# Where gate block 6's adding DMA stands in a hybrid encoder block, and the order in which two PSUM pools open

## The chip, the cores and the metric

The kernel runs on one core of one Trainium2 chip. The metric is the device time of one execution in microseconds (us); less is better. The engines are TensorE (PE, with its weight loads shown apart as PEld), VectorE (DVE), ScalarE (ACT), GpSimd (POOL) and SyncE (SP). Each works through its own list of instructions in order, and waits on semaphores where it needs something of another engine or of a DMA. SP, ACT and POOL also issue DMAs; in the trace the issuing of a DMA from SP or ACT has a lane with a q (SPq, ACTq).

## The reference: what is computed

One layer of an encoder block on x of 512 frames by 1024 channels, all in 32-bit floats. An input projection feeds two token mixers and their gates; then come an output projection, a layer norm, a gated feed-forward network with a causal convolution, and a second layer norm. Cut to what matters here:

```python
proj = x @ w_in[layer]
q_a, k_a, v_a, q_i, k_i, w_i, q_s, k_s, v_s, g_a, g_b = jnp.split(proj, IN_OFFSETS, axis=-1)
y_a = ... # sparse attention: an indexer picks 256 keys per query, 8 heads
y_s = ... # stick-breaking attention, 8 heads
gate_a = jax.nn.sigmoid(g_a + b_gates[layer, 0])
gate_b = jax.nn.sigmoid(g_b + b_gates[layer, 1])
merged = gate_a * (y_a @ w_branch_dsa[layer]) + gate_b * (y_s @ w_branch_sb[layer])
x = layer_norm(DEEPNORM_ALPHA * x + merged @ w_out[layer], ln1_g[layer], ln1_b[layer])
u, g = jnp.split(x @ w_ffn_in[layer], 2, axis=-1)
h = jax.nn.gelu(causal_dwconv(u, conv_w[layer], conv_b[layer])) * g
x = layer_norm(DEEPNORM_ALPHA * x + h @ w_ffn_out[layer], ln2_g[layer], ln2_b[layer])
```

## The kernel before

**Precision.** PE multiplies in a rounded format. So every 32-bit operand is split into a high half (rounded) and a low half (the rest), and every product is three matmuls: high by high, low by high, high by low. For a projection block of 128 output channels (`proj_t`, lines 230 to 232) that makes 24 matmuls: eight chunks of the input channels, and for each L230 (x high by weight high), L231 (x low by weight high) and L232 (x high by weight low).

**Splitting the weights.** The class `Stream` runs through one list of weight pieces (`order`), each 128 by 1024 numbers or 512 KB. SP loads a piece into one of three `raw` buffers (L72), ACT copies it rounded into `whi` (L103), and the low half `wlo` comes about in one of three ways. DVE or POOL subtracts (L110); or, for the 14 pieces listed in `DMA_LO`, ACT writes the negated high half into `wlo` (L106, "the negated half") and POOL then issues a DMA that loads the same piece once more from memory and adds it onto that (L107, "the adding DMA"). `whi` and `wlo` have three buffers each. Gate blocks 4, 5, 6 and 7 (gb4 to gb7, pieces 28 to 31) are done in this third way; so `wlo_30` is gate block 6's low half and `wlo_31` is gate block 7's.

**The attention stage** lasts from about 60 to 330 us. The two mixers' heads run one after the other: stick-breaking heads 0 to 7, then sparse heads 0 to 7. A head's own matmuls are few, and its chain on the other engines is long, so PE is filled between them with the projection blocks in the order of `FILL`: ... qa0 ka0 gb4 gb5 gb6 gb7 qa1 ka1 va ... For a stick-breaking head, PE makes `z_ps` (L530), ACT takes two sigmoids, `keep` and `beta` (L534, L535), DVE runs a reversed running product over `keep` (L544, "the sticks"), and POOL multiplies `beta` by it (L547, "the head's product"). From head 4 on the weights are turned round by DMA: ACT and POOL write the two 16-bit halves of `beta` into `keep` (L466, L467), SP issues two transposing DMAs into `pl` (L469), POOL and ACT put the halves together in `back` (L478, L479), ACT and DVE split that into `pth` and `ptl` (L481, L485), and PE multiplies these by the values (`av_ps`, L501). Beside this DVE works through the top-256 selection for the sparse heads (L420, L421, `score`). A sparse head starts with `l_ps` (L570).

**What sets the order.** The instructions are handed to a scheduler that simulates a timeline and fixes the order of each engine's list; `tc.issue_after(x)` ties what is issued inside it to come after instruction x in that order. Four ties stand around the change. POOL's product of a head is tied behind the adding DMA last recorded in `st.added` for head 5 alone (`behind=i == TURN + 1`, TURN being 4). ACT's copies of ka0 (`stack_hl`, L335 and L336) are tied behind `pth` of head 4 (`firsts[0]`). `Stream.behind` makes one coming high half wait for that same `pth`; that is gate block 6's. The sigmoid of gate block 4 (L627) has no tie.

**The last two PSUM pools.** PSUM has eight banks; pool `psB` holds banks 0 to 3 throughout, and `psA` holds 4 to 7 until the first two blocks of the feed-forward stage are done. These are u_ps and g_ps of blocks 0 and 1, made by `ffn_in` and read by `activate` (ACT copies u_ps, L964; DVE multiplies g_ps by the activated c, L977). Then `psA` is closed and its four banks go to two new pools, each tile waiting for what last stood in its own bank: `psC` (u_ps and g_ps of blocks 2 to 21) takes 4 and 5, and `psD` (the sums P0 and P1, L1001 to L1003) takes 6 and 7.

## Time and profile before

| what | value |
|---|---|
| timed runs of the kernel before | 752.59, 752.68, 753.98 us; median 752.68 |
| the profiled execution's own time | 753.88 us |
| its span, first to last instruction | 752.1 us |
| mean granted TensorE clock over the span | 0.994 |
| PE busy | 739.6 us, 98% of the span |
| DVE, ACT, POOL busy | 569.3, 406.4, 149.5 us |
| issue to landing of the 14 adding DMAs, median | 7.1 us |

Times on the profile's page and in the trace count from the start of the span. A row of the timeline reads: start in us, duration in us, engine, line, operation, out<-in, shape, number of instructions merged; in square brackets at its end stands how long the engine sat idle before it and what ended that. The waits view gives the total, the number and the longest of the waits of one kind. The windows view gives, for each stretch, its length and each engine's busy time in it (with the number of instructions), then the granted TensorE clock as a share of full speed, the DMA engines' mean share and GB/s. "DMA to landing" is the time from issue until a DMA's semaphore tells that all has landed, as minimum, median and maximum of those in the window.

### The profile page before, as it was taken

What the parts mean: (1) busy time and instruction counts of PE and PEld (TensorE: products, weight loads), DVE (VectorE), ACT (ScalarE), POOL (GpSimd) and SP (SyncE); (2) the same over time, 40 slices, a digit from 0 to 9 for tenths busy, and PEclk for the clock granted to TensorE, in tenths of its full rate; (3) what the DMA queues carried; (4) which work ended last, traced back from release to release, by engine and by line L of the source; (5) the groups of instructions that cost most, each with busy time, mean ns of one, the idle gap of its engine ahead of it and who ended that gap; (6) DMA issues with size and microseconds to landing.
All of it is one profiled execution on the core that took longest, in us unless ns stands there. A gap on an engine that the chain in (4) does not pass through costs nothing.

```text
span 752.1 us, 9760 instructions
## 1 busy us (share of the span) xinstructions
PE 739.6 (98%) x3485; PEld 619.5 (82%) x3485; DVE 569.3 (76%) x907; ACT 406.4 (54%) x572; POOL 149.5 (20%) x161
## 2 busy tenths in 40 slices
PE   9999999998999999999999999999999999999995
PEld 7877888886888888888889888888888888888885
DVE  5569788998579999658774967676776668668995
ACT  5465767795786588746374534443443344346430
POOL 1001224374742432000011111011101101110011
PEclk9999999999999999999999999999999999999998
DMA  8445887796556455327732444435343444448532
GB/s 268 151 127 183 190 183 170 151 203 162 133 152 161 122 146 118 121 61 231 303 60 75 170 143 158 146 114 167 125 159 136 140 141 143 141 146 290 198 117 84
DMA packets 71008, 116.38 MB, mean 155 GB/s; under 512 B 39913, under 2 KB 40169, under 8 KB 70961
## 3 DMA queue, kind: packets, MB, share of 16 engines
q1 hardware_dynamic: 63680, 93.33, 41.1%
q0 software_dynamic: 5744, 18.38, 9.7%
q10 hardware_dynamic: 1536, 4.06, 2.2%
q8 instruction: 27, 0.44, 0.3%
q14 instruction: 21, 0.16, 0.1%
HBM read 95.93 MB, written 9.98 MB: 141 GB/s over the span
## 4 chain that ended last, share of the span: by engine, by line
PE 92%; DVE 4%; DMA 1%; issue 1%; ACT 1%; POOL 0%; DVEq 0%; POOLq 0%; ACTq 0%
PE u_ps L922 5%; PE u_ps L921 5%; PE g_ps L922 5%; PE u_ps L923 5%; PE g_ps L921 5%; PE g_ps L923 5%; PE m L1002 2%; PE m L1001 2%; PE m L1003 2%; PE av_ps L501 2%; PE ga_ps L232 2%; PE ga_ps L231 2%; PE ga_ps L230 2%; PE o_ps L852 2%; PE o_ps L851 2%; PE o_ps L850 2%
## 5 line engine op out<-in xcount | busy, mean ns | idle before, releaser
L103 ACT ACTIVATE whi<-raw 128x1024 fp32r<-128x1024 f32 (+1 forms) x124 | 124.0, 1002 | 158.7 <-PE g_ps L922 45.9
L110 DVE TENSOR_TENSOR wlo<-raw,whi 128x1024 fp32r<-128x1024 f32 (+1 forms) x105 | 124.3, 1185 | 40.4 <-ACT whi L103 39.5
L923 PE MATMUL u_ps<-x1h,wlo 128*128 128x512 f32 (+1 forms) x192 | 71.4, 372 | 0.0
L921 PE MATMUL u_ps<-x1h,whi 128*128 128x512 f32 (+1 forms) x192 | 71.3, 372 | 0.0
L922 PE MATMUL u_ps<-x1l,whi 128*128 128x512 f32 (+1 forms) x192 | 71.3, 371 | 0.0
L921 PE MATMUL g_ps<-x1h,whi 128*128 128x512 f32 (+1 forms) x184 | 69.9, 380 | 0.0
L922 PE MATMUL g_ps<-x1l,whi 128*128 128x512 f32 (+1 forms) x184 | 69.9, 380 | 0.0
L923 PE MATMUL g_ps<-x1h,wlo 128*128 128x512 f32 (+1 forms) x184 | 69.9, 380 | 0.0
L921 PEld LDWEIGHTS u_ps<-x1h,whi 128*128 128x128 f32 x192 | 36.2, 188 | 6.3
L922 PEld LDWEIGHTS u_ps<-x1l,whi 128*128 128x128 f32 x192 | 36.2, 188 | 6.2
L923 PEld LDWEIGHTS u_ps<-x1h,wlo 128*128 128x128 f32 x192 | 36.2, 188 | 6.2
L921 PEld LDWEIGHTS g_ps<-x1h,whi 128*128 128x128 f32 x184 | 34.6, 188 | 6.6
L923 PEld LDWEIGHTS g_ps<-x1h,wlo 128*128 128x128 f32 x184 | 34.6, 188 | 6.5
L922 PEld LDWEIGHTS g_ps<-x1l,whi 128*128 128x128 f32 x184 | 34.6, 188 | 6.5
L944 DVE TENSOR_TENSOR t<-raw 128x512 f32<-128x512 f32 x11 | 7.6, 692 | 40.0 <-DMA raw<-in_w_fo_dram 39.6
L559 POOL TENSOR_TENSOR bm<-win,score 128x256 f32<-128x256 f32 (+2 forms) x24 | 26.0, 1112 | 32.2 <-DMA pl<-bm 16.1
L963 POOL MEMSET u<- 128x2 f32 x22 | 2.1, 98 | 145.0 <-ACT whi L103 101.2
L977 DVE TENSOR_TENSOR hF<-g_ps,c 128x512 f32<-128x512 f32 x22 | 15.1, 686 | 20.8 <-PE g_ps L923 20.8
L969 ACT ACTIVATE c<-c,cwt 128x512 f32<-128x512 f32 x22 | 15.9, 725 | 25.2 <-DVE c L968 25.0
L819 POOL TENSOR_TENSOR rstd<-rstd,mhalf 128x1 f32<-128x1 f32 x8 | 7.7, 958 | 104.4 <-DVE rstd L818 104.4
L232 PE MATMUL gb_ps<-xh,wlo 128*128 128x512 f32 x64 | 25.7, 404 | 2.6 <-DMA wlo<-in_w_t_dram 2.6
L420 DVE MAX8 m<-score 128x8 f32<-128x256 f32 (+2 forms) x48 | 26.5, 554 | 1.7 <-DMA pl<-keep 0.8
(578 smaller groups left out, 2085.2 us busy)
## 6 DMA issues: line engine op xcount, KB each, us to landing
raw<-in_w_fi_dram SPq DMA_DIRECT2D x44, 512.0 KB, 3.3
raw<-in_w_t_dram SPq DMA_DIRECT2D x32, 512.0 KB, 3.5
raw<-in_w_fo_dram SPq DMA_DIRECT2D x26, 512.0 KB, 4.1
wlo<-in_w_t_dram POOLq DMA_DIRECT2D x14, 512.0 KB, 7.1
raw<-in_w_br_dram SPq DMA_DIRECT2D x8, 512.0 KB, 4.0
raw<-in_w_o_dram SPq DMA_DIRECT2D x8, 512.0 KB, 4.4
raw<-in_w_v_dram SPq DMA_DIRECT2D x7, 512.0 KB, 3.8
raw_b<-in_w_fo_dram SPq DMA_DIRECT2D x6, 512.0 KB, 5.3
```

Of the source, the lines that this page charges most:

```text
L103: self.high = nc.scalar.activation(hi[:, :w], t[:, :w], AF.Copy).ins
L110: self.done[key] = eng.tensor_sub(lo[:, :w], t[:, :w], r32(hi[:, :w])).ins
L230: nc.tensor.matmul(ps[:M], wh[:, c], xh[k], start=(k == 0), stop=False)
L231: nc.tensor.matmul(ps[:M], wh[:, c], xl[k], start=False, stop=False)
L232: nc.tensor.matmul(ps[:M], wl[:, c], xh[k], start=False, stop=(k == KC - 1))
L420: nc.vector.max(m8, sc)
L559: nc.gpsimd.tensor_add(bm[:, OFF[j]:OFF[j] + N], win[:, 512 - N:512], score[j])
L921: nc.tensor.matmul(ps[:, c], wh[:, kc], x1h[:, k, c], start=(k == 0), stop=False)
L922: nc.tensor.matmul(ps[:, c], wh[:, kc], x1l[:, k, c], start=False, stop=False)
L923: nc.tensor.matmul(ps[:, c], wl[:, kc], x1h[:, k, c], start=False, stop=(k == KC - 1))
L969: nc.scalar.activation(c, c, AF.Gelu_apprx_tanh, bias=cwt[:, f, 3:4])
L977: nc.vector.tensor_mul(F[:, o:o + 2].rearrange("p a b -> p (a b)"), gps_, c)
```

## The change

`Stream` now keeps every negated half in `st.highs`, by piece. ACT's copies of ka0 and its sigmoid of gate block 4 are tied behind gate block 6's negated half, instead of ka0's copies behind head 4's `pth`. The high half after gate block 6's (gate block 7's) is tied behind that negated half too. POOL's product of head 5 is tied behind gate block 5's adding DMA, which is the same DMA as before; the product of head 6 is newly tied behind gate block 6's adding DMA. And `psD` is opened ahead of `psC`, and closed after it.

```diff
@@ class Stream
+        self.highs = {}
...
             if key in self.lo_by_dma:
-                self.high = nc.scalar.activation(lo[:, :w], r32(hi[:, :w]), AF.Copy, scale=-1.0).ins
-                self.done[key] = self.added = nc.gpsimd.dma_start(lo[:, :w], self.pieces[self.ns][1], accum_op=ALU.add).ins
+                self.high = self.highs[key] = nc.scalar.activation(lo[:, :w], r32(hi[:, :w]), AF.Copy, scale=-1.0).ins
+                if key == "gb6":
+                    self.behind = self.high
+                self.done[key] = nc.gpsimd.dma_start(lo[:, :w], self.pieces[self.ns][1], accum_op=ALU.add).ins
@@ sb_sticks
-    def sb_sticks(beta, keep, behind=False):
+    def sb_sticks(beta, keep, behind=None):
...
-        with tc.issue_after(st.added) if behind else nullcontext():
+        with tc.issue_after(st.done[behind]) if behind else nullcontext():
             nc.gpsimd.tensor_mul(beta, beta, keep[:, 1:ATT + 1])
@@ filler
             elif kind in ("ks", "ka"):
-                with tc.issue_after(firsts[0]) if t == "ka0" and firsts else nullcontext():
+                with tc.issue_after(st.highs["gb6"]) if t == "ka0" and firsts else nullcontext():
                     qk[t] = stack_hl(ps, "k", 4, t)
             elif kind == "gb":
                 g = xp.tile([128, 512], F32, tag="m", bufs=8, name=t)
-                ups[t] = nc.scalar.activation(g, ps, AF.Sigmoid, bias=bgt[:, 8 + n:9 + n]).ins
+                with tc.issue_after(st.highs["gb6"]) if n == 4 else nullcontext():
+                    ups[t] = nc.scalar.activation(g, ps, AF.Sigmoid, bias=bgt[:, 8 + n:9 + n]).ins
@@ advance
-        last = sb_sticks(*following, behind=i == TURN + 1)
+        last = sb_sticks(*following, behind={TURN + 1: "gb5", TURN + 2: "gb6"}.get(i))
@@ tile_block
     close(ac)
+    psd, psD = open_pool("psD", space=PSUM, reuse_waits="tile")
     psc, psC = open_pool("psC", space=PSUM, reuse_waits="tile")
-    psd, psD = open_pool("psD", space=PSUM, reuse_waits="tile")
...
+    close(psc)
     close(psd)
-    close(psc)
```

The ties move instructions on all five engines between about 160 and 240 us; before and behind that stretch the lists are the same but for a few DVE and ACT rows in the last 50 us. No instruction is added or removed. The line numbers of the changed kernel are up to four higher. The numbers behind the names tell buffers apart: `_30_` is gate block 6's piece and `_31_` gate block 7's, beta_1642 and keep_1643 are stick-breaking head 6's, pl_1574 and back_1718 head 5's planes, pl_1713 head 6's planes, pth_1839 and av_ps_1980 head 6's turned weights and their product.

The first place is ACT's list where gate block 6 is split, before:

```order
L103 ACTIVATE whi_30_1624<-raw_30_1622 128x1024
L335 ACTIVATE ka0a_1676<-ka0_ps_1629 64x512
L336 ACTIVATE ka0b_1677<-ka0_ps_1629 64x512
L103 ACTIVATE whi_31_1684<-raw_31_1682 128x1024
L627 ACTIVATE gb4_1755<-gb4_ps_1689,bgt_105 128x512
L106 ACTIVATE wlo_30_1625<-whi_30_1624 128x1024
L106 ACTIVATE wlo_31_1685<-whi_31_1684 128x1024
```

and in the change:

```order
L104 ACTIVATE whi_30_1624<-raw_30_1622 128x1024
L107 ACTIVATE wlo_30_1625<-whi_30_1624 128x1024
L338 ACTIVATE ka0a_1676<-ka0_ps_1629 64x512
L339 ACTIVATE ka0b_1677<-ka0_ps_1629 64x512
L104 ACTIVATE whi_31_1684<-raw_31_1682 128x1024
L631 ACTIVATE gb4_1755<-gb4_ps_1689,bgt_105 128x512
L107 ACTIVATE wlo_31_1685<-whi_31_1684 128x1024
```

Gate block 6's negated half passes the four instructions that stood between it and its high half; gate block 7's keeps its place behind gate block 4's sigmoid. POOL's list at the same place, before:

```order
L467 COPY keep_1525<-beta_1524 128x1280
L547 TENSOR_TENSOR beta_1642<-beta_1642,keep_1643 128x1280
L107 DMA wlo_30_1625<-in_w_t_dram 128x1024
L107 DMA wlo_31_1685<-in_w_t_dram 128x1024
L467 COPY keep_1643<-beta_1642 128x1280
L479 COPY back_1718<-pl_1574 128x1280
```

and in the change:

```order
L470 COPY keep_1525<-beta_1524 128x1280
L110 DMA wlo_30_1625<-in_w_t_dram 128x1024
L550 TENSOR_TENSOR beta_1642<-beta_1642,keep_1643 128x1280
L110 DMA wlo_31_1685<-in_w_t_dram 128x1024
L482 COPY back_1718<-pl_1574 128x1280
L470 COPY keep_1643<-beta_1642 128x1280
```

Gate block 6's adding DMA passes head 6's product; gate block 7's stays behind it. The second place is SP's list, which issues the loads and the transposing DMAs, before:

```order
L72 DMA raw_33_1857<-in_w_t_dram 128x1024
L72 DMA raw_34_1890<-in_w_v_dram 128x1024
L469 DMA_TRANSPOSE pl_1574<-keep_1525 128x10x128
L554 DMA win_2056<-s_win 128x512
L72 DMA raw_35_1924<-in_w_v_dram 128x1024
L72 DMA raw_36_2006<-in_w_v_dram 128x1024
L469 DMA_TRANSPOSE pl_1713<-keep_1643 128x10x128 x2
```

and in the change:

```order
L73 DMA raw_33_1857<-in_w_t_dram 128x1024
L472 DMA_TRANSPOSE pl_1574<-keep_1525 128x10x128
L73 DMA raw_34_1890<-in_w_v_dram 128x1024
L557 DMA win_2056<-s_win 128x512
L472 DMA_TRANSPOSE pl_1713<-keep_1643 128x10x128
L73 DMA raw_35_1924<-in_w_v_dram 128x1024
L472 DMA_TRANSPOSE pl_1713<-keep_1643 128x10x128
L73 DMA raw_36_2006<-in_w_v_dram 128x1024
```

Head 5's second transpose passes one load, and head 6's two pass two loads and one load. The third place is PE's list in the values of the sparse mixer (va_ps, 128 by 512 each), where head 6's turned weights are used; before, twenty-one matmuls of va stand ahead of the row of av_ps, of which these are the last:

```order
L269 MATMUL va_ps2_2094<-whi_34_1892,xl1_186 128x512
L267 MATMUL va_ps1_2093<-whi_35_1926,xh2_227 128x512
L267 MATMUL va_ps2_2094<-whi_35_1926,xh2_227 128x512
L501 MATMUL av_ps_1980<-pth_1839,vs0_704 128x384
L570 MATMUL l_ps_2067<-ka0b_1677,qa0b_1617 128x512 x2
L501 MATMUL av_ps_1980<-ptl_1840,vs0_704 128x384
```

and in the change seven:

```order
L271 MATMUL va_ps1_2093<-wlo_34_1893,xh0_131 128x512
L272 MATMUL va_ps1_2093<-whi_34_1892,xl0_132 128x512
L270 MATMUL va_ps0_2092<-whi_34_1892,xh1_185 128x512
L504 MATMUL av_ps_1980<-pth_1839,vs0_704 128x384
L573 MATMUL l_ps_2067<-ka0b_1677,qa0b_1617 128x512 x2
```

Head 6's product with the values passes fourteen matmuls of va. In the built programs the banks of the feed-forward stage differ too: before, u_ps and g_ps of block 1 stand in banks 4 and 5, block 2's u_ps in 4, and P0 and P1 in 6 and 7; in the change, u_ps and g_ps of block 1 stand in banks 5 and 4, block 2's u_ps in 6 (which block 0's u_ps had), and P0 and P1 in 4 and 5.

## The prediction

> **What bounds the kernel now.** I read the page's busy shares and its chain of waits first, then PE's waits, then the timeline at the longest of them.

> ```profile
> PE 739.6 (98%) x3485; PEld 619.5 (82%) x3485; DVE 569.3 (76%) x907; ACT 406.4 (54%) x572; POOL 149.5 (20%) x161
> ...
> PE 92%; DVE 4%; DMA 1%; issue 1%; ACT 1%; POOL 0%; DVEq 0%; POOLq 0%; ACTq 0%
> ```

> PE is busy for 98% of the span. So an edit that adds or removes no matmul can only move what is left: the stretches in which PE stands or runs slowly. The view of PE's waits lists all of them:

> ```profile
> PE gb_ps L232 <- DMA wlo<-in_w_t_dram: 2.6, 1, 2.6
> ...
> PE dot_ps L403 <- ACT relu L406: 1.0, 1, 1.0
> ```

> The one wait of 2.6 us is on the low half of gate block 6. PE's timeline there:

> ```profile
> 170.28 0.39 PE L230 MATMUL gb_ps<-xh,whi 128*128 128x512 f32 x1
> 170.50 0.39 PE L231 MATMUL gb_ps<-xl,whi 128*128 128x512 f32 x1
> 173.46 0.80 PE L232 MATMUL gb_ps<-xh,wlo 128*128 128x512 f32 x1 [2.57 <-DMA wlo<-in_w_t_dram]
> ...
> 176.19 0.60 PE L232 MATMUL gb_ps<-xh,wlo 128*128 128x512 f32 x1
> 176.61 0.41 PE L230 MATMUL gb_ps<-xh,whi 128*128 128x512 f32 x1
> ```

> Starts of such matmuls lie 0.22 to 0.23 us apart (170.28 to 170.50). The L232 that starts at 173.46 would have started at 170.73, so 2.73 us are lost. The seven matmuls from 173.46 to 176.61 take 3.15 us instead of 7 x 0.227 = 1.59, another 1.56 us. The windows view says why:

> ```profile
> 52.00:54.00 2.00, 0.98 (x8) 0.79 (x7) 1.90 (x3) 2.00 (x5) 0.00 (x0) 1.00 0.57 154
> ...
> 170.50:173.40 2.90, 0.39 (x2) 0.00 (x0) 2.83 (x6) 2.90 (x7) 1.24 (x1) 0.97 1.09 215
> 173.40:176.80 3.40, 3.34 (x8) 2.66 (x9) 3.40 (x7) 0.74 (x2) 0.17 (x1) 0.52 0.24 46
> ```

> After the stall the granted clock is 0.52. After the 1.0 us wait near 53 us it stays 1.00, so a short wait costs its own length alone. The stall is worth 2.73 + 1.56 = **4.29 us**, the most that the change can win there.

> **The adding DMA comes earlier.** What makes the low half late stands in ACT's and POOL's timelines (whi at 160.73 is gate block 6's, 162.88 gate block 7's, the L106 pair at 164.55 their negated halves; L547 at 162.24 is head 6's product):

> ```profile
> 150.92 1.04 ACT L106 ACTIVATE wlo<-whi 128x1024 fp32r<-128x1024 f32 x1
> ...
> 160.73 1.04 ACT L103 ACTIVATE whi<-raw 128x1024 fp32r<-128x1024 f32 x1
> 161.68 0.57 ACT L335 ACTIVATE ka0a<-ka_ps 64x512 fp32r<-64x512 f32 x1
> ...
> 162.88 1.06 ACT L103 ACTIVATE whi<-raw 128x1024 fp32r<-128x1024 f32 x1
> ...
> 164.55 2.00 ACT L106 ACTIVATE wlo<-whi 128x1024 fp32r<-128x1024 f32 x2
> ```

> ```profile
> 142.61 2.45 POOL L547 TENSOR_TENSOR beta<-beta,keep 128x1280 f32<-128x1280 f32 x1 [4.00 <-DVE keep L544]
> ...
> 152.26 0.88 POOL L107 DMA_DIRECT2D wlo<-in_w_t_dram  x1 [1.13 <-ACT wlo L106]
> 152.94 2.70 POOL L547 TENSOR_TENSOR beta<-beta,keep 128x1280 f32<-128x1280 f32 x1
> ...
> 156.91 1.46 POOL L467 COPY keep<-beta 128x1280 uint16<-128x1280 uint16 x1
> 162.24 3.55 POOL L547 TENSOR_TENSOR beta<-beta,keep 128x1280 f32<-128x1280 f32 x1 [3.87 <-DVE keep L544]
> 165.91 1.80 POOL L107 DMA_DIRECT2D wlo<-in_w_t_dram  x2
> ```

> Both halves of the change are needed. With the negated half moved alone, POOL would still be in the product until 165.79; with the DMA moved alone, it would wait for a half that ends at 165.6. Together: the high half ends at 161.77, the negated half follows at 161.80 and takes 1.05, to 162.85. POOL takes the DMA 0.30 after such a half (151.96 to 152.26), at **163.15**, 2.76 us earlier than 165.91. POOL has been idle since 158.37, so nothing holds it up. How long it takes to land, from the views of wlo for gate block 6's DMA alone, for it and gate block 7's, and for the ten from 100 to 200 us:

> ```profile
> DMA to landing us min/median/max: 7.5/7.5/7.5
> ...
> DMA to landing us min/median/max: 7.5/8.3/9.1
> ...
> DMA to landing us min/median/max: 5.2/7.2/9.1
> ```

> Issued at 163.15 it lands at 170.65 if it takes 7.5 as now, and PE wants it at 170.73: just in time. The bounds are 5.2 (168.4, early) and 9.1 (172.25, a wait of 1.5 us). I take 7.2 to 7.5, its own time and the median: the 9.1 is that of a second DMA issued 0.87 behind a first, and gate block 6's has no other adding DMA beside it now. Wait left over: 0 to 1.5, taken as 0.1.

> **What it is moved past.** Head 6's product starts after the DMA instead of at 162.24: 163.15 + 0.68 (152.26 to 152.94) = 163.83, 1.6 us later. It takes between 2.45 (row of 142.61) and 3.55 (now), so it ends between 166.3 and 167.4 instead of 165.79. Behind it on POOL stand gate block 7's DMA, the put-together of head 5's planes and head 6's low plane. Gate block 7's negated half keeps its place and ends about 0.1 later than the pair's end of 166.55, so POOL can issue from 167.0; with the product that is 167.0 to 167.4, against 166.78 now. Landing takes 7.2 when alone and 9.1 behind another: 174.2 to 176.5. PE needs it 22 matmuls behind the first low half of gate block 6: 170.73 + 22 x 0.227 = 175.72. Wait: 0 to 0.8, taken as 0, since the two adding DMAs are now 4 us apart. A late gate block 6 pushes this need back too, so the two bounds do not add.

> On ACT, ka0's copies, gate block 7's high half and gate block 4's sigmoid start about 1.05 us later (161.68 becomes 162.76). Nobody wants them soon: ka0 is first used at 188.9, gate block 7's first matmul at 170.05, gate block 4's result only with the branch products. The load into the raw buffer that gate block 7's high half frees goes 1 us later; that piece is used at 198.6. All covered by PE's 10 us of gate blocks 4 and 5.

> **The later heads.** When PE comes 4 us earlier, the sparse heads' chain must come as well. It hangs on head 6's planes, whose transposes stood behind two loads on SP:

> ```profile
> 176.50 0.33 SPq L554 DMA_DIRECT2D win<-s_win  x1
> 177.62 5.16 SPq L72 DMA_DIRECT2D raw<-in_w_v_dram  x2
> 182.94 3.61 SPq L469 DMA_TRANSPOSE pl<-keep  x2
> ...
> 199.50 1.49 DVE L485 TENSOR_TENSOR ptl<-back,pth 128x1280 fp32r<-128x1280 f32 x1 [1.43 <-ACT pth L481]
> ...
> 203.40 0.34 PE L501 MATMUL av_ps<-pth,vs 128*128 128x384 f32 x1
> ```

> PE uses head 6's weights at 203.40, and they are ready at 200.99. In the change fourteen matmuls of va that stood ahead come behind: 203.40 - 4.2 - 14 x 0.227 = 196.0. That is 5.0 us too early for 200.99. But the first transpose now follows the load of win directly: 176.9 instead of 182.94, 6 us earlier before any of PE's gain, which puts the weights at about 195. So no wait here, by 1 us or more.

> Then comes a stretch in which DVE has little room:

> ```profile
> 176.80:205.00 28.20, 28.20 (x134) 23.81 (x134) 18.49 (x33) 19.03 (x26) 19.64 (x14) 1.00 0.63 159
> 226.00:260.00 34.00, 34.00 (x160) 28.29 (x158) 32.01 (x46) 22.19 (x31) 12.26 (x12) 1.00 0.59 140
> ```

> DVE (third pair of figures) is busy for 32.01 of 34.00 us. If its work does not start earlier, it can catch up 2.0 us and PE gives back 4.2 - 2.0 = 2.2. But it starts with PE's results, which come earlier, and idles 9.7 of 28 us between 176.8 and 205; I take 0.2, between 0 and 2.2.

> **The pools.** The rows of block 1's last reader, of block 2's u_ps and of the first P:

> ```profile
> 421.35 0.39 PE L921 MATMUL u_ps<-x1h,whi 128*128 128x512 f32 x1
> ...
> 423.63 0.68 DVE L977 TENSOR_TENSOR hF<-g_ps,c 128x512 f32<-128x512 f32 x1
> ...
> 426.79 0.39 PE L1001 MATMUL P<-whi,ah 128*128 128x512 f32 x1
> ```

> Block 1's g_ps is free at 424.31 and sits in bank 4 in the change. In the old order of opening, block 2's u_ps would take bank 4 and wait 3.0 us from 421.35. In the new one P0 takes it, at 426.79, 2.5 us after it is free. So this edit costs and wins nothing against before; it keeps the moved banks from costing.

> **Sum.** 4.29 - 0.1 (gate block 6) - 0 (gate block 7) - 0.2 (DVE) = 4.0 us. The profiled execution would go from 753.88 to 749.9. Its own time is 1.20 above the median of the timed runs, 752.68; I take the gain off the median: **748.7 us**.

> **Rivals.** *(a) The timed runs do not pay the slow clock.* The three runs are 752.59, 752.68 and 753.98, the profiled one 753.88; the step of 1.3 is near the 1.56 of the slow stretch. If the faster runs stall without it, they gain 2.73 - 0.3: 750.2. For it: that step. Against: a row of one execution cannot tell, and other things vary too. [...]

> *(b) The adding DMA still lands late*, in 9.1 us, because head 5's second transpose now leaves next to it. The wait is 1.5 us, perhaps with some slow clock (0 to 1.56): 752.68 - (4.29 - 1.5 - 0.8) = 750.7.

> *(c) DVE gives back 2.2 us* between 226 and 260: 752.68 - (4.19 - 2.2) = 750.7.

> *(d) Nothing changes*, because the scheduler's other moves open waits that add up to the gain: 752.7. The trace shows none that large.

> *(e) Slower.* Head 6's planes stay where they were in time (pl has one buffer, and its readers on POOL and ACT were moved too), while PE asks for them 14 matmuls earlier: it waits 200.99 - 196.0 = 5.0 us, and after a stall of that length the clock drops for another 1.56. 752.68 - 4.2 + 6.6 = 755.1. It decides as soon as the weights come less than 2.4 us earlier than now. Against it stands SP's order.

> **Chances and range.** Forecast 0.57, (a) 0.12, (b) 0.12, (c) 0.07, (d) 0.06, (e) 0.06. The forecast's own range is 748.0 to 749.6: at best all 4.29 and a few tenths of smaller waits, at worst 1 us given back. To hold 8 in 10 the range must take in (a) and most of (b) and (c): 747.9 to 751.2. A difference of 0.2% (1.5 us) is about what a measurement of this kernel can tell; faster by more than that is below 751.2. Faster: the forecast, (a) and most of (b) and (c), 0.84. Same: (d) and the rest, 0.10. Slower: 0.06.

> **What would show it.** Right: PE's waits no longer list L232 on wlo, or under 0.5 us; the granted clock is 1.00 from 60 us to the tail; POOL issues gate block 6's DMA near 163.2 and gate block 7's near 167.2, each landing in 7 to 7.5; the span is about 748. Wrong: a wait of PE over 1 us on wlo (b), on ptl (e) or on P; PE idle between 226 and 260 with DVE ahead of it (c); or a span that falls by 4 while the timed runs fall by 2.5 (a).

## The result, and the profile after

The changed kernel took 750.60 us (median of six, 750.11 to 750.99); the kernel before 754.51 (median of six, 752.59 to 756.15; the three executions of the table above are among them). The ratio is 0.995 (95% interval 0.9932 to 0.9969). In two later sets (experiments 6 and 7) it was 0.994 (0.9925 to 0.9954) and 0.9963 (0.995 to 0.9977). Over all sets the kernel before has a median of 755.01 in 72 executions (751.88 to 756.57), the changed one 750.63 in 17 (749.95 to 751.63). The change is faster by about 4 us (4.4 by these medians, 2.8 to 4.5 by the three ratios), and it takes most of the spread away.

The profiled execution of the changed kernel took 750.56, its span is 748.7. Its page's busy shares, and then PE's waits:

```profile
PE 738.1 (99%) x3485; PEld 618.5 (83%) x3485; DVE 569.8 (76%) x907; ACT 406.7 (54%) x572; POOL 148.1 (20%) x161
```

```profile
PE idle_ps L210 <- DVE idle L207: 1.2, 1, 1.2
PE dot_ps L406 <- ACT relu L409: 1.0, 1, 1.0
PE bs_ps L605 <- DVE wlo L113: 0.5, 1, 0.5
PE bs_ps L603 <- DVE ka2b L341: 0.2, 1, 0.2
```

The wait on gate block 6's low half is gone. In its place stand two small ones on DVE in the branch products (`bs_ps`), which the first profile of before did not have. The timelines of ACT, POOL and PE at the place, the landing of the two adding DMAs, and the windows view over it (the pairs are PE, PEld, DVE, ACT and POOL, the last three figures the granted clock, DMA share and GB/s):

```profile
160.96 1.04 ACT L104 ACTIVATE whi<-raw 128x1024 fp32r<-128x1024 f32 x1
162.03 1.06 ACT L107 ACTIVATE wlo<-whi 128x1024 fp32r<-128x1024 f32 x1
```

```profile
163.40 0.87 POOL L110 DMA_DIRECT2D wlo<-in_w_t_dram  x1 [4.80 <-ACT wlo L107]
164.00 2.75 POOL L550 TENSOR_TENSOR beta<-beta,keep 128x1280 f32<-128x1280 f32 x1
167.22 0.88 POOL L110 DMA_DIRECT2D wlo<-in_w_t_dram  x1 [0.47 <-ACT wlo L107]
```

```profile
DMA to landing us min/median/max: 7.4/7.4/7.4
...
DMA to landing us min/median/max: 7.1/7.1/7.1
```

```profile
170.73 0.39 PE L234 MATMUL gb_ps<-xl,whi 128*128 128x512 f32 x1
170.96 0.39 PE L235 MATMUL gb_ps<-xh,wlo 128*128 128x512 f32 x1
```

```profile
169.50:176.50 7.00, 7.00 (x33) 5.70 (x32) 6.94 (x13) 6.53 (x10) 2.03 (x3) 1.00 0.54 135
226.00:260.00 34.00, 33.29 (x158) 27.57 (x157) 32.02 (x45) 18.82 (x26) 12.68 (x12) 1.00 0.55 140
```

Gate block 6's DMA goes out at 163.40 and has landed 7.4 later, at about 170.8. PE uses the half at 170.96, 0.23 behind the matmul ahead of it: no wait, with about 0.2 us to spare. In six profiles with this order of the lists the half landed before its use, by less than 0.4 us, and in the seventh (two pieces on POOL) PE does not wait for it either. PE is busy for all 7.00 us, at full clock.

To see where time comes from and goes, I divide each profiled execution at the same matmuls: the first of the gate blocks (97.56 in the kernel before), the first and the last of the stick-breaking branch products (225.79 and 265.66) and the first P (426.79). Times are differences of their starts in PE's timeline; the kernels other than the first two belong to the experiments below.

| kernel | gate blocks to branch products | the branch products | to the first P |
|---|---|---|---|
| before | 128.23 | 39.87 | 161.13 |
| changed | 124.02 | 40.60 | 161.14 |
| before, again | 127.13 | 40.96 | 161.14 |
| pools alone | 128.17 | 40.79 | 161.14 |
| negated half alone | 125.51 | 39.29 | 161.14 |
| product alone | 128.10 | 39.35 | 161.13 |
| changed without the pools | 123.99 | 40.83 | 165.99 |
| changed, second and third time | 124.02, 124.01 | 40.62, 41.13 | 161.13, 161.14 |
| changed, a piece on POOL, twice | 123.99, 123.99 | 40.03, 40.38 | 161.14, 161.13 |
| changed, two pieces on POOL | 124.16 | 39.86 | 161.84 |
| before, a piece on POOL | 126.99 | 39.42 | 161.13 |

The first stage falls by 4.21 us, the second grows by 0.73, the third is the same. Against the second profile of the kernel before, which has no slow stretch (experiment 1), the first stage falls by 3.11 and the second by 0.36. Behind the first P all of them agree within 0.2 us.

### The profile page after: what moved, and what is told of

The parts are those of the page before. It is cut to its first block, busy times and chain, and to the rows that moved or that the text cites. A ratio compares the mean times of both kernels' runs of the same rounds, so it can differ in the third digit from the quotient of the medians.

```text
span 748.7 us, 9765 instructions
## 1 busy us (share of the span) xinstructions
PE 738.1 (99%) x3485; PEld 618.5 (83%) x3485; DVE 569.8 (76%) x907; ACT 406.7 (54%) x572; POOL 148.1 (20%) x161
## 4 chain that ended last, share of the span: by engine, by line
PE 89%; DVE 4%; issue 2%; ACT 2%; POOL 1%; DMA 0%; DVEq 0%; ACTq 0%; POOLq 0%
PE u_ps L926 5%; PE u_ps L927 5%; PE g_ps L926 5%; PE g_ps L927 5%; PE u_ps L925 5%; PE g_ps L925 5%; PE m L1006 2%; PE m L1005 2%; PE m L1007 2%; PE av_ps L504 2%; PE ga_ps L235 2%; PE ga_ps L234 2%; PE gb_ps L235 2%; PE gb_ps L234 2%; PE gb_ps L233 2%
## 5 line engine op out<-in xcount | busy, mean ns | idle before, releaser
L550 POOL TENSOR_TENSOR beta<-beta,keep 128x1280 f32<-128x1280 f32 x8 | 21.6, 2705 | 26.1 <-DVE keep L547 20.9
```

Source lines behind the costliest of these rows:

```text
L550: nc.gpsimd.tensor_mul(beta, beta, keep[:, 1:ATT + 1])
```

## Experiment 1: the kernel before, again

No edit. It stands for the question of rival (a): does every execution pay the slow clock?

> The kernel before, run again beside itself, with span and mean granted clock of every execution. The slow stretch of 3.4 us at half clock takes 0.0023 off the mean clock of the span (3.413 x 0.5 / 752). My theory: every execution stalls on gate block 6's low half and pays the slow clock, so each clock is near 0.994 and each time between 752.5 and 756, ratio 1.000 within 0.002. Rival (a): the slow clock is paid in some executions only; then the clocks fall into two groups, near 0.994 and near 0.997, the second about 1.6 us faster.

Measured: 754.15 us (twelve executions, 753.14 to 756.82), ratio 0.9996 (0.9985 to 1.0007). PE's waits, and the windows view divided at steps of 3.41 us (see the last section):

```profile
PE gb_ps L232 <- DMA wlo<-in_w_t_dram: 3.0, 1, 3.0
...
PE bs_ps L602 <- DVE wlo L110: 1.0, 1, 1.0
```

```profile
169.14:172.56 3.42, 2.28 (x13) 1.63 (x11) 2.48 (x7) 3.18 (x7) 1.98 (x2) 1.00 1.12 224
172.56:175.97 3.41, 1.57 (x7) 1.31 (x8) 3.41 (x7) 2.17 (x5) 0.00 (x0) 1.00 0.70 139
175.97:179.38 3.41, 3.41 (x17) 2.83 (x16) 3.38 (x6) 0.00 (x0) 2.17 (x1) 1.00 0.27 78
```

The stall is longer here (3.0 us instead of 2.6), and yet the clock stays at 1.00. So not every execution pays the slow clock: the premise of (a) holds, and my theory, that each pays, falls. In this pair of profiles nothing is won by it: the execution without it gets 1.10 us back in the first stage (127.13 instead of 128.23) and loses 1.09 in the second (40.96 instead of 39.87), where DVE now owes PE a low half. Nor do the twelve times fall apart cleanly by their mean clock: 753.30 has 0.994, 755.57 has 0.996.

More executions show more. Of the thirteen profiles, the four with a slow stretch ahead of the tail have a mean clock of 0.994 to 0.996, the nine without one 0.996 to 0.998. So, by these profiles, I take a clock of 0.997 and above for an execution without it and 0.995 and below for one with it; 0.996 can be either. The kernel before was timed 66 times beside the experiments, with its clock on record:

| mean granted clock | executions | median us | from, to |
|---|---|---|---|
| 0.997, 0.998 | 15 | 753.32 | 752.62, 755.11 |
| 0.996 | 24 | 755.03 | 751.88, 755.73 |
| 0.992 to 0.995 | 27 | 755.29 | 753.96, 756.57 |

The slow stretch goes with about 2.0 us, near the 1.56 that (a) put on it. The second profile, at 754.41, is one of the longer executions without it. All seventeen executions of the changed kernel lie at 0.996 to 0.998.

## Experiment 2: the change without the pools

```diff
-    psd, psD = open_pool("psD", space=PSUM, reuse_waits="tile")
     psc, psC = open_pool("psC", space=PSUM, reuse_waits="tile")
+    psd, psD = open_pool("psD", space=PSUM, reuse_waits="tile")
```

(and the two closed in the old order)

> The changed kernel with psC opened ahead of psD again; every engine's list is the same as in the changed kernel, only the banks differ. My theory: block 2's u_ps stands in the bank of block 1's g_ps, and waits from 418.11 until DVE has read that (row of 420.65, until 421.33): 3.2 us, and about 1.5 us of slow clock behind it. The time goes up by 4.7 from 750.6 to about 755.3, ratio to the kernel before 1.001. Rival: the order of the pools is worth nothing (a wait under 0.3 us), ratio 0.995 as with the whole change.

Measured: 755.49 us, ratio 1.0002 (0.9991 to 1.0014). Its longest wait of PE, and the windows behind it:

```profile
PE u_ps L925 <- DVE hF L981: 3.0, 1, 3.0
```

```profile
419.06:422.47 3.41, 1.08 (x5) 0.90 (x6) 3.34 (x6) 1.20 (x3) 0.09 (x1) 1.00 0.39 119
422.47:425.89 3.42, 3.42 (x10) 2.66 (x9) 2.38 (x4) 1.51 (x2) 0.00 (x0) 0.50 0.65 265
```

With the old order of opening, block 2's u_ps waits 3.0 us for DVE to read block 1's g_ps, and the next 3.4 us run at half clock: the third stage is 4.85 us longer. That is all of the gain. In the trace every engine's list is the same as in the changed kernel, so the banks alone do it. Of the twelve executions, the three at a clock of 0.997 took 752.81 to 753.89 and the other nine (0.993 to 0.996) 754.43 to 756.67, so here too the slow stretch does not come every time. The line that nobody would call a part of the DMA's move decides whether the change is worth anything.

## Experiment 3: the pools alone

In the kernel before:

```diff
+    psd, psD = open_pool("psD", space=PSUM, reuse_waits="tile")
     psc, psC = open_pool("psC", space=PSUM, reuse_waits="tile")
-    psd, psD = open_pool("psD", space=PSUM, reuse_waits="tile")
```

> The kernel before with psD opened ahead of psC and nothing else; all lists stay the same. My theory: with the old lists no tile waits for its bank in either order, so the ratio is 1.000 within 0.001 and the stall on gate block 6 is as before. Rival: the other order is worth something by itself, ratio 0.999 or less, and a part of the change's gain is its.

Measured: 754.48 us, ratio 0.9998 (0.9983 to 1.0013). PE's waits are those of before: 2.4 us on gate block 6's low half, and 0.7 and 0.2 in the branch products.

```profile
PE gb_ps L232 <- DMA wlo<-in_w_t_dram: 2.4, 1, 2.4
...
PE bs_ps L600 <- DVE ka2b L338: 0.7, 1, 0.7
PE bs_ps L602 <- DVE wlo L110: 0.2, 1, 0.2
```

The lists are those of the kernel before here, too. The order of the pools wins nothing by itself; it keeps the banks that the scheduler moved from costing 4.85 us. It also shows that the small waits on DVE are in executions of the kernel before, too.

## Experiment 4: the negated half alone

```diff
-        last = sb_sticks(*following, behind={TURN + 1: "gb5", TURN + 2: "gb6"}.get(i))
+        last = sb_sticks(*following, behind={TURN + 1: "gb5"}.get(i))
```

> The changed kernel without the new tie of head 6's product; POOL's list has that product ahead of gate block 6's adding DMA again, while ACT's negated half stays behind its high half. My theory: both parts are needed. The product starts at 162.24 and takes 2.75 to 3.55, so the DMA goes out between 165.0 and 165.8, lands 7.1 to 7.5 later (172.1 to 173.3), and PE, which wants it at 170.96, stands 1.1 to 2.3 us; with the slow clock behind it or not the gain over the kernel before is 0.4 to 3.2 us, time between 751.7 and 754.1, ratio 0.996 to 0.9995. Rival: the negated half alone does it (POOL is early enough), no wait on wlo, ratio 0.995.

Measured: 752.99 us (751.18 to 753.97), ratio 0.9969 (0.9956 to 0.9981). In the profiled execution, the fastest of them, POOL's rows, the landing of the two DMAs, and PE's wait:

```profile
162.80 3.55 POOL L550 TENSOR_TENSOR beta<-beta,keep 128x1280 f32<-128x1280 f32 x1 [3.87 <-DVE keep L547]
166.29 0.87 POOL L110 DMA_DIRECT2D wlo<-in_w_t_dram  x1
167.55 0.86 POOL L110 DMA_DIRECT2D wlo<-in_w_t_dram  x1 [0.40 <-ACT wlo L107]
```

```profile
DMA to landing us min/median/max: 6.3/7.0/7.7
```

```profile
PE gb_ps L235 <- DMA wlo<-in_w_t_dram: 1.2, 1, 1.2
```

As expected POOL is in the product until about 166.3, so the DMA goes out at 166.29, 2.89 us later than in the changed kernel; it landed in 6.3 us here, and PE stood 1.2 us; an execution of median length lies 1.8 us above this one. The ratio lies inside what was expected; it is not the 0.995 of the rival. The profiled execution has no slow stretch; the five of the nine that have a clock of 0.994 or 0.995 took 752.99 to 753.97, the other four 751.18 to 752.44. Leaving out the tie moved more than the product: the scheduler drew up PE's, DVE's and ACT's lists anew, and the branch products take 39.29 us here without a wait on DVE.

## Experiment 5: the product alone

```diff
-                if key == "gb6":
-                    self.behind = self.high
...
-                with tc.issue_after(st.highs["gb6"]) if t == "ka0" and firsts else nullcontext():
+                with tc.issue_after(firsts[0]) if t == "ka0" and firsts else nullcontext():
...
-                with tc.issue_after(st.highs["gb6"]) if n == 4 else nullcontext():
-                    ups[t] = nc.scalar.activation(g, ps, AF.Sigmoid, bias=bgt[:, 8 + n:9 + n]).ins
+                ups[t] = nc.scalar.activation(g, ps, AF.Sigmoid, bias=bgt[:, 8 + n:9 + n]).ins
```

> The changed kernel without the ties on ACT: gate block 6's negated half is again behind ka0's copies, gate block 7's high half and gate block 4's sigmoid, but head 6's product is tied behind gate block 6's adding DMA. My theory: POOL waits for the half until 165.6 and issues the DMA near 165.9 as before, PE stands 2.6 to 2.8 us with the slow clock behind it, and head 6's product now ends near 169.3 instead of 165.8, so nothing is won and up to 1 us may be lost: 754 to 755.5, ratio 0.999 to 1.002. Rival: the product ahead of the DMA was what made it late; then the ratio is near 0.995.

Measured: 753.71 us, ratio 0.9976 (0.9964 to 0.9988). POOL's rows, PE's wait and the windows:

```profile
166.29 0.87 POOL L108 DMA_DIRECT2D wlo<-in_w_t_dram  x1 [7.54 <-ACT wlo L107]
166.90 2.75 POOL L548 TENSOR_TENSOR beta<-beta,keep 128x1280 f32<-128x1280 f32 x1
```

```profile
PE gb_ps L233 <- DMA wlo<-in_w_t_dram: 2.3, 1, 2.3
```

```profile
170.70:174.11 3.41, 1.09 (x5) 0.62 (x4) 3.38 (x3) 3.41 (x8) 2.58 (x2) 1.00 1.05 199
174.11:177.52 3.41, 3.41 (x9) 2.64 (x9) 3.41 (x8) 1.47 (x2) 0.59 (x1) 0.50 0.19 36
```

The mechanism is the expected one: POOL stands idle for 7.54 us and issues the DMA no earlier than before, PE waits 2.3 us and runs 3.4 us at half clock. But I had expected no gain, and it is 0.24%. The stages say where it is: the first is 128.10, as before; the branch products take 39.35, with no wait on DVE, where the executions of before took 39.87 to 40.96. The scheduler had drawn up other lists here, as in experiment 4: the next low half that DVE makes behind the first branch product starts 3.01 us after it (2.29 in experiment 4), where it starts 5.09 to 6.41 us after it in the three profiles with the lists of before. Here the mean clocks form two groups with no overlap: seven executions at 0.995 took 753.45 to 754.18, four at 0.997 took 750.63 to 752.29. The slow stretch again goes with about 2 us.

So either part alone wins something (0.31% and 0.24%), neither wins what the whole does, and only the whole removes the stall. How much of the two small gains is the part's own and how much comes of the new lists is not told apart.

## Experiment 6: the two small waits in the branch products

DVE's timeline of the changed kernel ahead of its wait, POOL's beside it, and PE's row:

```profile
213.55 1.79 DVE L113 TENSOR_TENSOR wlo<-raw,whi 128x1024 fp32r<-128x1024 f32 x1 [3.61 <-ACT whi L104]
...
227.48 2.32 DVE L113 TENSOR_TENSOR wlo<-raw,whi 128x1024 fp32r<-128x1024 f32 x1
...
231.25 1.20 DVE L113 TENSOR_TENSOR wlo<-raw,whi 128x1024 fp32r<-128x1024 f32 x1
```

```profile
225.69 3.02 POOL L562 TENSOR_TENSOR bm<-win,score 128x256 f32<-128x256 f32 x3 [4.84 <-DVE va L250]
...
229.85 0.50 PE L605 MATMUL bs_ps<-ys0h,wlo 128*128 128x512 f32 x1 [0.55 <-DVE wlo L113]
```

DVE sits idle 3.61 us for a high half of ACT's (213.55), and the subtraction that PE waits for takes 2.32 beside POOL's three products (225.69 to 228.71), while one of the same size takes 1.20 at 231.25, where POOL is idle (228.71 to 239.98). Whether POOL's products are what makes it longer is not shown.

Neither is new. The first profile of the kernel before has the same idle time (3.53 us, ended at 216.12) and the same long subtraction (2.31 us at 230.88), and no wait. What differs is when PE asks. Counted from the first gate block, this subtraction starts at 133.32, 133.54 and 133.56 us in the three profiles with the lists of before (before, again, pools alone) and at 129.69, 129.49 and 129.53 in those of the changed kernel. So DVE comes 3.6 to 4.1 us earlier with the change. PE comes 4.21 earlier than in the first profile, where it ran through the slow stretch, and so meets DVE's late half; in the second profile of before it comes 1.10 earlier without any edit, and meets it too.

The edit gives the subtraction of 213.55 to POOL, which is idle from 214.34 to 216.81; it was put in the changed kernel and in the kernel before:

```diff
-POOL_LO = "ks1 va0 va1 va2 va3".split()
+POOL_LO = "ks1 va0 va1 va2 va3 bs0".split()
```

The changed kernel once more, beside them:

> The changed kernel again, on the same chip as the next three, with the mean clock of every execution. My theory: with no stall the clock cannot drop, so the executions lie close together, 750.0 to 751.2, ratio 0.994 to 0.9955, each clock 0.996 to 0.998. Rival: the adding DMA is only just in time and misses in some executions; then some lie 1 to 3 us higher with a clock near 0.994.

> The changed kernel with one DVE subtraction (the low half of the first piece of the stick-breaking branch, row of 213.55, 1.79 us) given to POOL, which stands idle then (214.34 to 216.81). PE's and ACT's lists stay the same. My theory: what was given back, a wait of 0.55 us on the next piece's low half at 229.85 and 0.2 us at 256.6, is DVE being behind by its own load, so 1.2 to 1.8 us less work ahead of it takes the wait at 229.85 away: 0.4 to 0.7 us faster than the changed kernel, 749.9 to 750.2. Rival: DVE waits for ACT's pth at 221.78 (idle 1.01 ahead of it) and is paced by ACT, not by its load; then the wait and the time stay as they are.

> The kernel before with the same subtraction given to POOL; PE's and ACT's lists stay the same. My theory: an execution whose clock stays at full after the stall (as the second profile of the kernel before) gets its 1.5 us back and gives 1.0 of it away again at the low half that DVE owes; so the slow clock shows little in the times. With DVE relieved that wait goes: the undisturbed executions (clock 0.996 and up) come down by about 1 us, those with the slow stretch by 0 to 0.3, median 0.3 to 0.8 us below the kernel before, ratio 0.999 to 0.9996. Rival: DVE's wait there has nothing to do with its load; ratio 1.000, the wait of 1.0 us on wlo at bs_ps stays.

Measured on one chip: the changed kernel 750.38 us (749.95 to 750.72), ratio 0.994 (0.9925 to 0.9954), each clock 0.996 to 0.998 (that the clock cannot drop without a stall was my estimate and is not shown); with the piece on POOL 749.92 (749.53 to 750.83), ratio 0.9937 (0.9921 to 0.9952); the kernel before with the piece on POOL 754.00, ratio 0.9992 (0.9978 to 1.0006). PE's waits in the branch products, of the changed kernel and then with the piece on POOL:

```profile
PE bs_ps L603 <- DVE ka2b L341: 0.4, 1, 0.4
PE bs_ps L605 <- DVE wlo L113: 0.3, 1, 0.3
```

```profile
PE bs_ps L603 <- DVE ka2b L341: 0.2, 1, 0.2
```

The wait on the low half goes, and the stage falls by 0.59 us (40.62 to 40.03), as expected. In the times the two overlap. In the kernel before, the profile with the piece on POOL has neither the wait nor the slow stretch, but the first profile of before had no such wait either. Whether the executions without the slow stretch came down and the others not can't be told from twelve: at a clock of 0.997 and above they took 752.22 to 754.10, at 0.995 and below 753.10 to 756.95, and the interval holds 1. That the slow clock's cost is hidden under DVE's lateness is seen in one pair of profiles (experiment 1). Against it stand the profile of the pools alone, which has both the slow stretch and the waits on DVE, and the 2 us between the timed executions with and without the slow stretch. Why the branch products take 39.87 to 40.96 us with one and the same list stays open.

## Experiment 7: the two small waits once more

```diff
-POOL_LO = "ks1 va0 va1 va2 va3".split()
+POOL_LO = "ks1 va0 va1 va2 va3 bs0 qa3".split()
```

and the two kernels to compare it with on the same chip:

> The changed kernel once more, as the measure for the next two on the same chip: 750.0 to 751.0, ratio 0.994.

> The changed kernel with the low half of the branch's first piece on POOL, once more, since its six executions (median 749.92) overlapped those of the changed kernel (750.38). My theory: DVE's load sets the wait at 229.85, the profile shows the stretch from the first branch product to the last 0.6 us shorter (40.03 instead of 40.62), so the median is again 0.4 to 0.7 below the changed kernel's. Rival: the difference was the spread of six executions; medians within 0.2.

> As the run before, and the subtraction of the piece qa3 (2.31 us on DVE at 252.50, ahead of ka2's copies) is POOL's too, which is idle from 256.8 to 263.5. PE's and ACT's lists stay the same. My theory: the wait of 0.2 to 0.4 us at 256 on ka2b goes as well, the stretch between the first and the last branch product falls from 40.03 to 39.3 to 39.8, and the time is another 0.2 to 0.6 us lower, 749.3 to 749.8. Rival: POOL is late with it (PE wants it at 262.8), PE waits there up to 1 us, and the time is that of the changed kernel or more.

Measured: the changed kernel 751.24 us (750.64 to 751.63), ratio 0.9963, above the 750.0 to 751.0 expected; bs0 on POOL 750.62 (749.58 to 751.44), ratio 0.9957 (0.9942 to 0.9972); bs0 and qa3 on POOL 750.44 (750.38 to 751.49), ratio 0.9957 (0.9943 to 0.9971). PE's waits with both on POOL:

```profile
PE l_ps L573 <- DVE ka3a L340: 0.5, 1, 0.5
PE bs_ps L605 <- DVE wlo L113: 0.3, 1, 0.3
```

With bs0 on POOL the median is below the changed kernel's on both chips, by 0.46 and 0.62 us, as the stage is in the profiles (by 0.59 and 0.75); single executions overlap, so this is likely, not certain. With qa3 on POOL too the wait on ka2b goes from the branch products (39.86 us for the stage), but 0.3 us on the low half is there again, and 0.5 us on ka3a comes behind them, where the third stage takes 161.84 instead of 161.13: nothing more is won, and the 749.3 to 749.8 expected were missed. The version with bs0 alone is the one that I would keep.

## Why the prediction was right, and where it was not

- **The stall: 4.29 us, less 0.1.** Right against an execution that pays the slow clock: 4.21 us between the first gate block and the first branch product. Against one that does not (experiment 1, a wait of 3.0 us) it is 3.11; the prediction's stall without the slow stretch was 2.73. The DMA was put at 163.15 and went out at 163.40, in an execution whose first gate block began 0.23 later (97.79); it took 7.4 of the 7.2 to 7.5. "Just in time" is what the rows show, about 0.2 us to spare. None of the changed kernel's seventeen executions (749.95 to 751.63) has a clock of 0.995 or less.
- **What it is moved past: nothing.** Right. Head 6's product ran at 164.00 (predicted 163.83) in 2.75 us, gate block 7's DMA went out at 167.22 (167.0 to 167.4) and landed in 7.1 us, at 174.3, ahead of its need. (Before, it went out at 166.85, not at the 166.78 of the prediction; nothing hangs on it.)
- **Both halves of the change are needed.** Right for the stall: 1.2 us of wait stay with the one and 2.3 with the other. Not foreseen: each alone also won time, 0.31% and 0.24%. The branch products are shorter in both, with lists that the scheduler drew up otherwise; that the lists are the reason is likely, not shown.
- **Head 6's planes: no wait.** Right. SP's, DVE's and PE's rows:

```profile
176.28 1.54 SPq L472 DMA_TRANSPOSE pl<-keep  x1
...
192.18 2.60 DVE L488 TENSOR_TENSOR ptl<-back,pth 128x1280 fp32r<-128x1280 f32 x1
...
196.15 0.34 PE L504 MATMUL av_ps<-pth,vs 128*128 128x384 f32 x1
```

  The transpose was put at 176.9, the weights at about 195 and PE's use at 196.0; they came at 176.28, 194.78 and 196.15.
- **DVE from 226 to 260: 0.2, between 0 and 2.2.** The mechanism, that DVE comes earlier nearly with PE, is right: 3.6 to 4.1 us earlier (experiment 6). The size can't be told from the profiles: the stage grows by 0.73 us against the first profile, 0.5 of it in a wait on a low half and 0.2 on ka2b (PE is busy for 33.29 of the 34.00 us). But the three profiles of the changed kernel (40.60, 40.62, 41.13) overlap with the three that have the lists of before (39.87, 40.96, 40.79).
- **The pools: nothing against before.** Right, and the price of leaving them out as well: a wait of 3.0 us, and with the slow clock behind it, which the prediction did not name there, 4.85 in that profile.
- **The sum in the profile's frame:** 749.9 predicted, 750.56 measured. Of the 0.66, 0.53 are the longer branch products and 0.23 a later start; 0.16 were won behind the first P, and the small rest lies in the stall and between time and span. The agreement is with the first profile of before, a short one among those that pay the slow clock (their median is 755.29).
- **The predicted time, 748.7, is 1.9 us too low,** and the step that failed is the last one: "I take the gain off the median of the timed runs, 752.68". The 4.0 us held 1.56 of slow clock, and the median was very likely that of an execution without it: the clocks of those three are not on record, but of the 27 later executions with a clock of 0.995 or less none took less than 753.96. Three executions were a poor base in another way too. Of the 72 timed in all, only five took less than 752.70, two of them among the first three, and the median is 755.01. The profiled execution's own 753.88 would have given 749.9. The forecast's own range, 748.0 to 749.6, was missed; the wide one held, by the room made for rival (a) and others and not by the forecast's own sum.
- **Rival (a), the slow clock,** given 0.12, is the one that the runs bear out. Not all executions pay it, those without it are about 2.0 us shorter (experiment 1), and its 750.2 is nearer to the measured 750.60 than the forecast. Its sign showed as well: the span fell by 3.4 us and the timed median by 2.1 against the three first runs. From 753.32 and 755.29, the medians without and with the slow stretch, to the changed kernel's 750.63 are 2.7 and 4.7 us, close to the prediction's 2.73 and 4.29. (b), (d) and (e) did not come; whether (c) came with some tenths of its 2.2 us is not shown.

## What to carry to other kernels

When a scheduler or an allocator stands behind an edit, ask what else it will draw up anew: here the banks alone would have eaten the whole gain (4.85 us in the third stage). A stall that went with a landing time (2.4 us of wait at 7.4, 3.0 at 7.9), and behind which the clock fell to half in two of the four profiles with the order of before, showed as spread (751.88 to 756.57 us in 72 executions); three runs do not give the base to subtract a gain from, and with the stall gone most of the spread went (749.95 to 751.63 in 17). Put the mean granted clock beside every time: here it sorted the executions (median 753.32 us at 0.997 and above, 755.29 at 0.995 and below), and a cost read in a profile is taken off executions that pay it. When PE comes earlier by some microseconds, look for the next engine that works its list in order and waits in it, and try giving one of its instructions to an engine that is idle just there; here that likely won half a microsecond.

## What the runs showed of the hardware

```profile
169.81:173.22 3.41, 1.08 (x5) 0.56 (x3) 3.00 (x7) 3.23 (x8) 1.62 (x1) 1.00 1.06 208
173.22:176.63 3.41, 3.17 (x8) 2.49 (x9) 3.41 (x7) 0.93 (x2) 0.00 (x1) 0.50 0.32 62
```

```profile
170.62:174.04 3.42, 2.18 (x10) 1.49 (x9) 3.42 (x5) 3.37 (x7) 0.60 (x1) 1.00 1.04 193
174.04:177.45 3.41, 3.41 (x17) 2.82 (x16) 3.38 (x8) 1.80 (x3) 0.61 (x1) 1.00 0.16 31
```

```profile
743.25:746.66 3.41, 1.24 (x11) 1.03 (x9) 3.31 (x9) 0.00 (x0) 0.62 (x1) 1.00 0.41 154
746.66:750.07 3.41, 0.00 (x0) 0.00 (x0) 2.01 (x4) 0.00 (x0) 0.30 (x1) 0.50 0.39 137
```

```profile
739.48:742.89 3.41, 1.55 (x13) 1.34 (x12) 3.31 (x9) 0.00 (x0) 0.31 (x1) 1.00 0.41 154
742.89:746.30 3.41, 0.00 (x0) 0.00 (x0) 2.32 (x5) 0.00 (x0) 0.61 (x1) 1.00 0.29 105
```

Windows with PE busy for 1.00 us (pools alone), 1.08 and 1.09 (before, without the pools, product alone) and 1.24 (36% of the window) were followed by 0.50; windows with 1.55 (45%), 1.57 (experiment 1), 1.71 (before with a piece on POOL) and 2.18 (negated half alone) by 1.00, and so was every one with 2.40 and more in the profiles of before and of the changed kernel. Between 1.24 and 1.55 us of 3.41 none of these windows lies. A wait of 2.3 us that falls into one window (product alone, PE busy for 1.09 of the 3.41) was followed by half clock, and one of 3.0 us that is split over two (experiment 1, PE busy for 2.28 and 1.57) was not. With the order of before, the clock fell to 0.50 behind the stall in two of the four profiles (before, 2.6 us of wait, and the pools alone, 2.4) and stayed at 1.00 in two (experiment 1, 3.0, and before with a piece on POOL, 2.8).

**How long an adding DMA takes.** Gate block 6's 512 KB landed in 7.2 to 7.4 us (six profiles with the order of the change), 7.3 (product alone) and 6.3 (negated half alone, with a second adding DMA 1.26 us behind it). With a second one issued directly behind, the first took 7.4 to 7.9 and the second 8.9 to 9.5 (the four profiles with the order of before). So the second is the one that took clearly longer; whether the first is held up by its company is not shown, and why it took only 6.3 once stays open.
